# Seven products in every gate/up and down stage of a two-layer encoder trunk, and the rotary angles on GpSimd

## The chip, the cores and the metric

One core of one Trainium2 chip runs the whole program. The metric is the device time of one execution in microseconds (us), as the median of several runs of the same program. A time belongs to the program from its launch to its end; the profile of one execution has a span, from its first to its last instruction, which is a little shorter.

The engines are called as in the profile: PE is TensorE's matmul, PEld its weight load, DVE is VectorE, ACT is ScalarE, POOL is GpSimd, SP is SyncE, whose queue (SPq) issues every DMA of this kernel.

## The reference

Two layers on a sequence of 256 frames, model width 1024, all in float32. Each layer is a half-step feed-forward block, a mixer, and a second half-step feed-forward block:

```
def rmsnorm(x, g):  y = x * rsqrt(mean(x * x) + EPS);  return y * g
def swiglu(h, w_gate, w_up, w_down):                       # D_FF = 2816
    return (silu(h @ w_gate) * (h @ w_up)) @ w_down

for i in range(2):
    x = x + 0.5 * swiglu(rmsnorm(x, ffn1_norm[i]), ...)
    h = rmsnorm(x, mix_norm[i]);  q_s, k_s, v_s, q_m = split(h @ w_in[i])
    o_m = memory attention of q_m over mem (256 rows, 4 heads)
    o_s = chunked attention with relative bias    (i = 0)
        | differential attention with rotary      (i = 1)
    x = x + concat([o_s, o_m]) @ w_out[i]
    x = x + 0.5 * swiglu(rmsnorm(x, ffn2_norm[i]), ...)
```

The rotary tables need cos and sin of position times inverse frequency. Only layer 1's mixer uses them.

## The kernel before

**Precision by splitting.** A product of two float32 matrices is made of three passes of a faster format. Every operand is split into `hi` (rounded) and `lo` (the rest), and `dense()` (lines 489 to 506) issues three matmuls: `xh*wh` (L496), `xh*wl` (L499) and `xl*wh` (L502), each 128 x 128 against 128 x 512. Three such matmuls are called one dense step below. ACT makes `hi` (L326 for weights) and DVE makes `lo` (L344), so each weight that comes in costs work on both.

**Stages.** The four feed-forward blocks are (layer, block) = (0,1), (0,2), (1,1), (1,2). Each has a gate/up stage and a down stage. The gate/up stage has 11 groups of 256 columns. For each group there are two weight chunks (the two halves of the contraction), each holding 256 gate and 256 up columns; a chunk takes 8 dense steps (4 of k by 2 halves of the rows). `evac()` (from line 601) turns a finished group into `silu(gate) * up`, transposes it in blocks (L621), writes it to DRAM (`hd`, L627) and reads it back turned (`hr`, L632), and splits it into the operand `ht` (L641, L643). The down stage has 11 chunks of 8 dense steps, one for each group. Its last three chunks are run with the output quarter as the outer loop (lines 867 to 873), so that `finish()` (L577) can add one quarter to `x` and prepare the next stage's operand (`prep_half`, L531) while the others still run.

**Seven products for eight.** A block product of 2 x 2 blocks can be made of seven products instead of eight. The kernel has this in two places. In a gate/up stage, `PAIR` names a group; it and its successor form the 2 x 2 blocks, and `product()` (L799) runs seven products of 4 dense steps, so 28 instead of 32. For that, `pair_items()` (L385) needs sums of weight blocks (L338), `pair_forms()` (L746) sums of the activation's blocks, whose unrounded halves `y` are kept, and `pair_sums()` (L768) adds up the results. In a down stage, `SEVEN` names chunks: `seven_item()` (L377) makes four sums and seven splits of the chunk's four parts, `seven_forms()` (L648) the same of the activation, `seven()` (L675) runs 7 dense steps instead of 8, and `seven_sums()` (L686) adds four banks that all such chunks of a stage share into `x`, after the last of them. Before the change block (0,1) has neither.

**Buffers.** Raw weight chunks go through 3 buffers, split chunks through 4 (`whl`); a seven-product chunk takes two of the four, since it has seven parts. `Xt` is the transposed, split activation of a stage (two `xh` and two `xl` tiles); the next stage's is allocated ahead of the down stage (line 837). `g4` (12 slots) holds `ht` and its like, `g2` (19 slots) small tiles, and PSUM has 8 banks.

**Order of work.** Nothing is reordered at run time. The program is written out by `Flow` (L47), a small model of time with costs for each engine: PE work moves its clock by 0.216 for a matmul (`T_MM`), and generators ("threads") are resumed when their time has come. A generator that yields `flow.now + 3.0` places its next instruction that much later in the order. Idle threads (the weight loader, the two splitters, the rotary setup) are served after the others. `dense()` gives them a turn after each matmul. `calm` conditions let an instruction in only when the modelled DVE (or ACT) is free, or, with `SLACK`, nearly free. Each engine executes its instructions strictly in that written order; on a wrong guess of a transfer's time the engine waits, with all that is behind.

**Rotary setup.** `rope_setup()` (from L1057) waits until all small loads written so far have gone out, then runs one chain of small 128 x 64 steps on DVE (L1071 to L1116): position times frequency, the argument reduced by a constant in five pieces, each for a high and a low part. Every step waits until the modelled DVE is entirely free (`calm`, L1053). Two sines on ACT (L1119, L1120) and 16 steps on DVE (L1128, L1130) end it.

**Memory.** `memory_turn()` (L923) brings `mem` through DVE transposes to DRAM, `memory_prep()` (L949) reads it back and splits it, `memory_kv()` (L991) uses it right after block (0,1). POOL computes the `rsqrt` of all norms (L516) and the rotary products of layer 1 (L1219).

Of the kernel before, what the change touches and what calls it, by code (L numbers as in the profile page):

```python
# [12 lines left out]
F32 = mybir.dt.float32  # L13
F32R = mybir.dt.float32r
# [6 lines left out]
P = 128  # L21
# [121 lines left out]
def kernel(  # L143
# [101 lines left out]
    class Item:  # L245
# [3 lines left out]
        def __init__(self, raws, uses=8, w=1):  # L249
# [3 lines left out]
            self.n, self.frees, self.takes, self.gives = 1, 1, 0, 0  # L253
# [15 lines left out]
    hl_left = [NHL]  # L269
    dma_free = [2.3]  # L270
# [94 lines left out]
    SEVEN = {(0, 1): (), (0, 2): (1, 4, 6), (1, 1): (1, 4, 6), (1, 2): (1, 4, 7)}  # L365
    PAIR = {(0, 1): None, (0, 2): 3, (1, 1): 3, (1, 2): 3}
# [10 lines left out]
    def seven_item(it):  # L377
# [3 lines left out]
        it.n, it.uses, it.takes, it.gives = 2, 7, 4, 4  # L381
# [48 lines left out]
    def plan_ffn(l, nm, wg, wu, wd):  # L430
# [58 lines left out]
    def dense(ps, xh, xl, ready, c, need, start, stop):  # L489
# [14 lines left out]
        if c.uses == 0:  # L504
            hl_left[0] += c.n
        return flow.pe(T_MM)
# [88 lines left out]
    def ffn(l, nm, xt, gc_next):  # L595
# [5 lines left out]
        def evac(g, ps, end, gives=None):  # L601
# [27 lines left out]
            g2.give()  # L629
            yield g2.has()  # L630
# [206 lines left out]
        nxt = None if gc_next is None else Xt(nm == 2 and PAIR[l + 1, 1] is not None)  # L837
# [27 lines left out]
        if nm == 1:  # L865
            table_hint(AF.Exp)
        for tb in range(2):
# [81 lines left out]
    def memory_prep():  # L949
        yield g2.has(8)  # L950
# [102 lines left out]
    def calm(n, extra=0.0):  # L1053
        t = flow.dve(n, extra) + 0.3
        return lambda: flow.now >= t and flow.free["V"] <= flow.now

    def rope_setup():  # L1057
# [13 lines left out]
        nc.vector.tensor_copy(pf, pi)  # L1071
        yield calm(2)
        for tb in range(2):
            nc.vector.tensor_scalar(out=ang[:, tb * 32:(tb + 1) * 32], in0=invf, scalar1=pf[:, tb:tb + 1],
                                    scalar2=None, op0=ALU.mult)
            yield calm(n)
# [3 lines left out]
        nc.vector.tensor_copy(hi, hr.bitcast(F32))  # L1080
        yield calm(n)
        nc.vector.tensor_sub(lo, ang, hi)
        yield calm(n)
# [595 lines left out]
```

## Time and profile before

| | us |
|---|---|
| median of 3 runs | 961.64 |
| lowest, highest | 959.97, 965.21 |
| the profiled execution, its time | 962.03 |
| the profiled execution, its span | 960.3 |

| engine | busy, us | share of the span |
|---|---|---|
| PE | 948.0 | 99% |
| DVE | 806.0 | 84% |
| ACT | 577.8 | 60% |
| POOL | 63.1 | 7% |

The share is that of the whole span. A stage is read on its own: the windows of the trace give busy time for a stretch, the timeline gives single instructions with what ended the idle time before them (in brackets), and the list of waits says who waited for whom. Block (0,1) runs to about 192 us, layer 0's mixer to about 310, block (0,2) to about 495, block (1,1) to about 675, layer 1's mixer to about 775, and the rest is block (1,2).

### The profile page before, as it was taken

What the parts mean: (1) busy time and instruction counts of PE and PEld (TensorE: products, weight loads), DVE (VectorE), ACT (ScalarE), POOL (GpSimd) and SP (SyncE); (2) the same over time, 40 slices, a digit from 0 to 9 for tenths busy, and PEclk for the clock granted to TensorE, in tenths of its full rate; (3) what the DMA queues carried; (4) which work ended last, traced back from release to release, by engine and by line L of the source; (5) the groups of instructions that cost most, each with busy time, mean ns of one, the idle gap of its engine ahead of it and who ended that gap; (6) DMA issues with size and microseconds to landing.
All of it is one profiled execution on the core that took longest, in us unless ns stands there. A gap on an engine that the chain in (4) does not pass through costs nothing.

```text
span 960.3 us, 13252 instructions
## 1 busy us (share of the span) xinstructions
PE 948.0 (99%) x4489; PEld 776.9 (81%) x4489; DVE 806.0 (84%) x1532; ACT 577.8 (60%) x1100; POOL 63.1 (7%) x65
## 2 busy tenths in 40 slices
PE   8999999999999999999999999999999999999998
PEld 6888888888877888888888888887787788888886
DVE  6867777788877889979989988798989888997885
ACT  6655555566676656556646655554676866665651
POOL 1000000022110100000000000000334100000000
PEclk9999999999999999999999999999999999999999
DMA  8988868486435387786756678666541375688761
GB/s 275 332 256 273 278 229 274 154 272 210 158 107 174 92 262 226 233 289 221 234 184 201 219 231 263 221 234 224 187 165 45 126 223 183 211 258 261 240 230 44
DMA packets 169294, 204.02 MB, mean 212 GB/s; under 512 B 9674, under 2 KB 144395, under 8 KB 169227
## 3 DMA queue, kind: packets, MB, share of 16 engines
q1 hardware_dynamic: 169226, 203.18, 65.7%
q8 instruction: 35, 0.57, 0.2%
q14 instruction: 33, 0.26, 0.1%
HBM read 188.99 MB, written 14.16 MB: 212 GB/s over the span
## 4 chain that ended last, share of the span: by engine, by line
PE 87%; DVE 8%; DMA 2%; ACT 1%; SPq 1%; issue 1%; DVEq 0%; ACTq 0%
PE gu L502 14%; PE gu L499 14%; PE gu L496 14%; PE acc L496 8%; PE acc L502 8%; PE acc L499 8%; DVE lo L344 3%; PE pj L502 3%; PE pj L499 3%; PE pj L496 3%; PE pair_m L502 2%; PE pair_m L499 2%; PE pair_m L496 2%; PE xtp L509 1%; PE S L1320 1%; PE AV L1401 1%
## 5 line engine op out<-in xcount | busy, mean ns | idle before, releaser
L326 ACT CAST hi<-raw 128x512 fp32r<-128x512 f32 (+1 forms) x469 | 338.2, 771 | 160.9 <-DMA raw<-in_ffn_w_up_dram 43.4
L344 DVE TENSOR_TENSOR lo<-raw,hi 128x512 fp32r<-128x512 f32 (+1 forms) x469 | 393.0, 873 | 45.4 <-ACT hi L326 44.6
L502 PE MATMUL gu<-hi,xl 128*128 128x512 f32 x608 | 236.9, 390 | 0.0
L496 PE MATMUL gu<-hi,xh 128*128 128x512 f32 x608 | 236.8, 389 | 0.0
L499 PE MATMUL gu<-lo,xh 128*128 128x512 f32 x608 | 236.7, 389 | 0.0
L502 PEld LDWEIGHTS gu<-hi,xl 128*128 128x128 f32 x608 | 114.1, 188 | 23.7
L499 PEld LDWEIGHTS gu<-lo,xh 128*128 128x128 f32 x608 | 114.1, 188 | 23.6
L496 PEld LDWEIGHTS gu<-hi,xh 128*128 128x128 f32 x608 | 114.2, 188 | 23.5
L499 PE MATMUL acc<-lo,ht 128*128 128x512 f32 x280 | 110.1, 393 | 2.0 <-DVE lo L344 2.0
L496 PE MATMUL acc<-hi,ht 128*128 128x512 f32 x280 | 110.0, 393 | 0.0
L502 PE MATMUL acc<-hi,ht 128*128 128x512 f32 x280 | 109.9, 393 | 0.0
L502 PE MATMUL pj<-hi,xl 128*128 128x512 f32 x160 | 64.5, 403 | 0.0
L499 PEld LDWEIGHTS acc<-lo,ht 128*128 128x128 f32 x280 | 52.9, 189 | 13.7 <-DVE lo L344 2.9
L499 PE MATMUL pj<-lo,xh 128*128 128x512 f32 x160 | 63.6, 397 | 0.0
L496 PE MATMUL pj<-hi,xh 128*128 128x512 f32 x160 | 63.5, 397 | 0.0
L502 PEld LDWEIGHTS acc<-hi,ht 128*128 128x128 f32 x280 | 53.0, 189 | 11.0
L496 PEld LDWEIGHTS acc<-hi,ht 128*128 128x128 f32 x280 | 53.0, 189 | 10.9
L641 ACT CAST ht<-hr 128x512 fp32r<-128x512 f32 x35 | 21.7, 619 | 65.2 <-DMA hr<-hd 65.1
L326 ACT CAST hi<-wsum 128x512 fp32r<-128x512 f32 x84 | 49.2, 621 | 15.7 <-DVE wsum L338 12.3
L344 DVE TENSOR_TENSOR lo<-wsum,hi 128x512 fp32r<-128x512 f32 x84 | 53.0, 682 | 0.0
L610 ACT ACTIVATE sil<-gu,xr 128x256 f32<-128x256 f32 x76 | 35.7, 469 | 24.6 <-PE gu L502 24.1
L643 DVE TENSOR_TENSOR ht<-hr,ht 128x512 fp32r<-128x512 f32 x35 | 24.0, 687 | 26.1 <-ACT ht L641 26.0
(215 smaller groups left out, 1297.6 us busy)
## 6 DMA issues: line engine op xcount, KB each, us to landing
raw<-in_ffn_w_down_dram SPq DMA_DIRECT2D x176, 256.0 KB, 4.3
raw<-in_ffn_w_gate_dram SPq DMA_DIRECT2D x86, 512.0 KB, 4.6
raw<-in_ffn_w_up_dram SPq DMA_DIRECT2D x86, 512.0 KB, 5.7
raw<-in_w_in_dram SPq DMA_DIRECT2D x32, 512.0 KB, 5.9
hd<-hb SPq DMA_DIRECT2D x44, 256.0 KB, 4.9
hr<-hd SPq DMA_DIRECT2D x44, 256.0 KB, 3.7
raw<-in_w_out_dram SPq DMA_DIRECT2D x8, 1024.0 KB, 4.9
raw<-in_w_mem_kv_dram SPq DMA_DIRECT2D x4, 1024.0 KB, 5.6
```

The source lines that it names most:

```text
L326: nc.scalar.copy(out=it.part(0, q, w), in_=src())
L344: nc.vector.tensor_sub(it.part(1, q, w), src(), it.part(0, q, w).bitcast(F32))
L496: nc.tensor.matmul(out=ps, lhsT=xh, rhs=wh, start=start, stop=False)
L499: nc.tensor.matmul(out=ps, lhsT=xh, rhs=wl, start=False, stop=False)
L502: nc.tensor.matmul(out=ps, lhsT=xl, rhs=wh, start=False, stop=stop)
L509: nc.tensor.transpose(out=dst, in_=src, identity=flip if flipped else ident)
L610: nc.scalar.activation(sil, ps[tb][:, 0:256], AF.Silu, scale=xt.r[tb])
L641: nc.scalar.copy(out=hi, in_=src)
L643: nc.vector.tensor_sub(lo, src, hi.bitcast(F32))
L1320: nc.tensor.matmul(out=ss[e][:, pr, :nk], lhsT=q[rows, pr, :], rhs=k[rows, pr, :], start=i == 0, stop=i == len(passes) - 1)
L1401: nc.tensor.matmul(out=av[64 * e:64 * e + 64, pr, :], lhsT=vsrc(kb, pr, e), rhs=pts[e][:, pr, kb, :], start=(kb == 0), stop=(kb == nb - 1))
```

## The change

- `PAIR` of block (0,1) becomes 5, so that groups 5 and 6 run as seven products. `SEVEN` becomes (1, 5) there; in the other three it is (1, 4, 7), which it already was in (1,2), while (0,2) and (1,1) had (1, 4, 6).
- Of the seven-product chunks of a stage only the first still takes two split buffers. The others are "guests": four of their parts are in one split buffer, and the other three are in the tiles of `Xt`, which are free once the gate/up stage is done. One guest can be there at a time (`xt_room`), and the next stage's `Xt` is allocated after the down stage's eighth chunk.
- The last three down chunks are split in the order of parts 0, 2, 1, 3, unless they are seven-product chunks.
- The read-back `hr` of each group is placed 2.0 later in the order.
- All of the rotary chain ahead of the sines (95 steps) goes from DVE to POOL, with 0.25 as its cost in the model and no condition on DVE. The 16 steps behind the sines stay on DVE, with a looser condition.
- `memory_turn` has the looser condition too, and `memory_prep` waits until all four pieces of `mem` were written.

```diff
@@ class Item
-            self.n, self.frees, self.takes, self.gives = 1, 1, 0, 0
+            self.n, self.frees, self.takes, self.gives, self.guest = 1, 1, 0, 0, False
...
         def part(self, lo, q, w=1):
-            t = (self.lo if lo else self.hi)[q // 4]
-            return t[:, q % 4 * 512:(q % 4 + w) * 512]
+            ts = self.lo if lo else self.hi
+            if self.guest and q >= 4:
+                return ts[q // 2 - 1].rearrange("p k t -> p (k t)")[:, q % 2 * 512:(q % 2 + w) * 512]
+            return ts[q // 4][:, q % 4 * 512:(q % 4 + w) * 512]
@@ split_hi
-            yield lambda: hl_left[0] >= it.n and all(r.raw is not None for r in it.raws)
+            yield lambda: (hl_left[0] >= it.n and all(r.raw is not None for r in it.raws)
+                           and (xt_room[0] or not it.guest))
             hl_left[0] -= it.n
+            if it.guest:
+                xt_room[0] = False
...
+            if it.guest:
+                for x, ts in (("xh", it.hi), ("xl", it.lo)):
+                    ts += [xtp.tile([P, KT, P], F32R, tag=f"{x}{j}", name=f"g{x}{j}") for j in range(2)]
@@
-    SEVEN = {(0, 1): (), (0, 2): (1, 4, 6), (1, 1): (1, 4, 6), (1, 2): (1, 4, 7)}
-    PAIR = {(0, 1): None, (0, 2): 3, (1, 1): 3, (1, 2): 3}
+    SEVEN = {(0, 1): (1, 5), (0, 2): (1, 4, 7), (1, 1): (1, 4, 7), (1, 2): (1, 4, 7)}
+    PAIR = {(0, 1): 5, (0, 2): 3, (1, 1): 3, (1, 2): 3}
@@ plan_ffn
             if c in SEVEN[l, nm]:
-                seven_item(dn[-1])
+                seven_item(dn[-1], c != SEVEN[l, nm][0])
+            elif c >= NG - 3:
+                u = dn[-1].units
+                u[1], u[2] = u[2], u[1]
@@ evac
             g2.give()
+            yield flow.now + 2.0
             yield g2.has()
             hr = g2.take([P, 4, P], F32, "hr")
@@ ffn, ahead of the down stage
-        nxt = None if gc_next is None else Xt(nm == 2 and PAIR[l + 1, 1] is not None)
+        xt_room[0] = True
@@ ffn, after the eighth down chunk
+        assert xt_room[0]
+        xt_room[0] = False
+        nxt = None if gc_next is None else Xt(nm == 2 and PAIR[l + 1, 1] is not None)
@@ memory_turn, memory_prep
-                yield lambda: flow.free["V"] <= flow.now
+                yield lambda: flow.free["V"] <= flow.now + SLACK
...
-        yield g2.has(8)
+        yield lambda: len(memd) == 4 and g2.left >= 8
@@ rope_setup, each of its 95 steps ahead of the sines in this way
-                nc.vector.tensor_scalar(out=a, in0=part, scalar1=float(cval), scalar2=None, op0=ALU.mult)
-                yield calm(n)
+                nc.gpsimd.tensor_scalar(out=a, in0=part, scalar1=float(cval), scalar2=None, op0=ALU.mult)
+                yield flow.pool(0.25)
...
-                    yield calm(n)
+                    flow.dve(n, 0.06)
+                    t = flow.dve(n, 0.06) + 0.3
+                    yield lambda: flow.now >= t and flow.free["V"] <= flow.now + SLACK
```

More of the change, by code (lines that the diff above doesn't have):

```diff
@@ L269 @@
     hl_left = [NHL]
+    xt_room = [False]
     dma_free = [2.3]
@@ L375, with seven_item @@
     WO = (0, 1, 2, 3)
-    def seven_item(it):
+    def seven_item(it, guest):
         r = [it.own(q) for q in range(4)]
         t = lambda j: lambda: it.t[j]
-        it.n, it.uses, it.takes, it.gives = 2, 7, 4, 4
+        it.n, it.uses, it.takes, it.gives, it.guest = 1 if guest else 2, 7, 4, 4, guest
         it.sums = [(r[1], r[0]), (r[3], t(0)), (r[3], r[1]), (r[2], t(1))]
@@ L505, in dense @@
             hl_left[0] += c.n
+            xt_room[0] |= c.guest
         return flow.pe(T_MM)
@@ L1079, in rope_setup @@
         yield flow.act(n)
[L1080 to L1083 removed]
+        nc.gpsimd.tensor_copy(hi, hr.bitcast(F32))
+        yield flow.pool(0.25)
+        nc.gpsimd.tensor_sub(lo, ang, hi)
+        yield flow.pool(0.25)
         def frac(dst, src):
[L1086 to L1089 removed]
+            nc.gpsimd.tensor_scalar(out=b, in0=src, scalar1=MAGIC, scalar2=MAGIC, op0=ALU.add, op1=ALU.subtract)
+            yield flow.pool(0.25)
+            nc.gpsimd.tensor_sub(dst, src, b)
+            yield flow.pool(0.25)
         left = Fraction(TWO_PI_INV_NUM, TWO_PI_INV_DEN)
@@ L1110, in rope_setup @@
                     yield from frac(fa, a)
-                    nc.vector.tensor_add(acc, acc, fa)
-                    yield calm(n)
+                    nc.gpsimd.tensor_add(acc, acc, fa)
+                    yield flow.pool(0.25)
                     yield from frac(acc, acc)
         S2PI = 6.283185
-        nc.vector.tensor_scalar(out=a, in0=acc, scalar1=0.25, scalar2=None, op0=ALU.add)
-        yield calm(n)
+        nc.gpsimd.tensor_scalar(out=a, in0=acc, scalar1=0.25, scalar2=None, op0=ALU.add)
+        yield flow.pool(0.25)
         yield from frac(a, a)
```

28 lines of the change are left out of this document (10 added, 18 removed).

## The prediction, made before the changed kernel was run

> **What bounds the kernel now.** I read the page's busy times first, then PE's matmuls in the timeline, then PE's waits, then the windows by stage.
>
> ```profile
> span 960.3 us, 13252 instructions
> PE 948.0 (99%) x4489; PEld 776.9 (81%) x4489; DVE 806.0 (84%) x1532; ACT 577.8 (60%) x1100; POOL 63.1 (7%) x65
> ```
> ```profile
> 400.34 0.39 PE L496 MATMUL gu<-hi,xh 128*128 128x512 f32 x1
> ...
> 401.02 0.39 PE L496 MATMUL gu<-hi,xh 128*128 128x512 f32 x1
> ```
>
> A busy PE is not yet a PE at its peak, so the pitch matters. Between these two L496 lie an L499 and an L502, so three matmuls take 401.02 - 400.34 = 0.68 us, that is 0.227 us each and 0.68 us for one dense step. PE keeps this pitch nearly everywhere. In the list of its waits (total, times, longest) the first line here is the end of block (1,1)'s down stage, the other three lie in the mixers:
>
> ```profile
> PE acc L499 <- DVE lo L344: 2.0, 2, 1.2
> ...
> PE ptp L509 <- DVE pe L1447: 0.6, 1, 0.6
> PE acc L496 <- DVE oT L1308: 0.4, 1, 0.4
> PE qktp L509 <- DVE m L1226: 0.4, 1, 0.4
> ```
>
> That stage's end in the timeline, and DVE's load by stage (length, then PE, PEld, DVE, ACT and POOL busy, granted clock, transfers' share, GB/s):
>
> ```profile
> 656.58 0.39 PE L496 MATMUL acc<-hi,ht 128*128 128x512 f32 x1
> 658.13 0.50 PE L499 MATMUL acc<-lo,ht 128*128 128x512 f32 x1 [1.17 <-DVE lo L344]
> ...
> 659.94 0.69 PE L499 MATMUL acc<-lo,ht 128*128 128x512 f32 x1 [0.85 <-DVE lo L344]
> ...
> 662.99 0.63 PE L502 MATMUL acc<-hi,ht 128*128 128x512 f32 x1
> 663.42 0.43 PE L496 MATMUL acc<-hi,ht 128*128 128x512 f32 x1
> 663.69 0.39 PE L499 MATMUL acc<-lo,ht 128*128 128x512 f32 x1
> ```
> ```profile
> 24.00:120.00 96.00, 96.00 (x424) 79.24 (x423) 68.96 (x98) 53.02 (x82) 0.00 (x0) 1.00 0.91 285
> 120.00:192.00 72.00, 72.00 (x325) 59.60 (x325) 53.93 (x142) 40.13 (x80) 2.59 (x4) 1.00 0.67 219
> 336.00:432.00 96.00, 96.00 (x425) 79.54 (x424) 86.71 (x141) 53.84 (x82) 0.00 (x0) 1.00 0.79 252
> 432.00:504.00 72.00, 72.00 (x327) 59.61 (x326) 66.71 (x127) 43.14 (x80) 1.38 (x2) 1.00 0.67 213
> 648.00:672.00 24.00, 21.99 (x93) 17.42 (x92) 19.37 (x32) 11.50 (x22) 0.00 (x0) 0.93 0.70 227
> ```
>
> PE waits twice for a weight's `lo` from DVE, 2.0 us in all, and then its matmuls start 0.43 apart (662.99 to 663.42) up to there, while the granted clock of that window is 0.93 instead of 1.00. Thirteen matmuls lie between 656.58 and 663.69: 7.11 us, where 13 x 0.227 = 2.95 would do. The stall costs 4.2 us: half of it is waiting, half the slow matmuls behind. The Trainium skill (TensorE: Matmul & The Clock Gate, Part 1) puts the fall to half clock down to an idle window of about 3.4 us; by that, these two waits cost their own 2.0 us alone, and the sum below would be 955.9. The trace disagrees: waits of 1.17 and 0.85 us went before the halved pitch. So PE bounds the kernel, DVE comes next, and one DVE stall is in the way.
>
> **Products.** Block (0,1) is the one without seven products. Its pair takes 7 x 4 = 28 dense steps for 32, and its two down chunks 7 for 8 each: 6 dense steps, 18 matmuls, 6 x 0.68 = **4.1 us** of PE. In the other three blocks the count is the same (three chunks before and after). PE is the bound, so this comes off the end if nothing else is late.
>
> What feeds it costs DVE. For the pair, block (0,2)'s gate/up window, which has one, is the comparison: 86.7 us of DVE in 96, against 69.0 in block (0,1). The price is so 17.7 us, and DVE stays at 87 of 96 (memory's transposes are in the 69.0 already). In (0,2) PE ran 96.00 of 96.00 with it. The pair's four operand forms are due only at group 5, and the halves `y` exist from the stage's start. For the down stage:
>
> ```profile
> L344 DVE TENSOR_TENSOR lo<-raw,hi 128x512 fp32r<-128x512 f32 x303 | 194.8, 686 | 23.7 <-ACT hi L326 23.6
> L338 DVE TENSOR_TENSOR wsum<-raw,wsum 128x512 f32<-128x512 f32 x42 | 27.9, 682 | 0.2
> L690 DVE SCALAR_TENSOR_TENSOR x<-msum,x 128x512 f32<-128x512 f32 x12 | 8.3, 688 | 0.2
> L657 DVE TENSOR_TENSOR sf<-hr 128x128 f32<-128x128 f32 x18 | 5.0, 278 | 0.0
> L1088 DVE TENSOR_TENSOR ropew<-ropew 128x64 f32<-128x64 f32 x20 | 4.4, 221 | 0.2
> ```
>
> Each seven-product chunk adds 4 sums and 3 splits (7 x 0.68 = 4.8), 4 forms (1.1) and two more, narrower `ht` splits (0.28 to 0.69 each, some 0.7 together): 6.6 us; the final sums are 8 steps of 0.69, 5.5. For two chunks 2 x 6.6 + 5.5 = 18.7 us. The rotary chain gives back, in 120 to 192, by the timeline, 38 of its 95 steps at 0.2 = 7.6. So 53.9 + 18.7 - 7.6 = 65 us of DVE in 72: tight, not over.
>
> **The rotary chain on POOL.** Over the whole span DVE loses 95 x 0.2 = 19 us of work. No POOL step of 64 columns stands in the trace; the nearest:
>
> ```profile
> L1219 POOL TENSOR_TENSOR m<-qkn,ropeS 128x256 f32<-128x256 f32 x12 | 11.2, 954 | 7.2 <-ACT hi L326 3.0 <-DVE rs L1439 2.0 <-ACT k L1252 1.2
> L200 POOL TENSOR_SCALAR_AFFINE_SELECT flip<-flip 128x128 f32<-128x128 f32 x1 | 0.3, 292 | 0.1
> ```
> ```profile
> 121.67 0.16 DVE L1071 CAST pos_f<-pos_i 128x2 f32<-128x2 int32 x1
> 173.07 1.28 ACT L878 ACT_TABLE_LOAD   x1
> 189.91 0.55 POOL L516 TENSOR_TENSOR xr<-v,nhalf 128x1 f32<-128x1 f32 x1 [66.34 <-DVE v L514]
> ```
>
> Bounds for one step: 0.29 (one input, twice the columns) and 0.95 (two inputs, four times the columns). I take 0.4, an estimate nearer the first, as the columns are half of its and more than half of the chain has one input. How the chain is written out sets its pace: each step is resumed 0.25 + 0.22 = 0.47 later in the model, and the model looks every 0.216, so after three matmuls, 3 x 0.227 = 0.68 us on the chip. From about 121 us that makes 95 x 0.68 = 65 us, to about 186. At 0.4 POOL keeps up, is done before `xr` is due at 190, and the sines find their input. They then fall behind the load of the other function table at 173, so two more loads of 1.28 may come, 0 to 2.6 us of ACT; ACT is busy 40 of 72 there, and 32 dense steps of `memory_kv` (22 us) that need no new `x` cover it. If that cover were gone, it would be 2.6 us of PE.
>
> POOL can also slow DVE:
>
> ```profile
> L1222 DVE TENSOR_TENSOR m<-qkn,ropeC 128x512 f32<-128x512 f32 x6 | 5.9, 988 | 0.0
> L1226 DVE TENSOR_TENSOR m<-m,m 128x512 f32<-128x512 f32 x6 | 4.1, 684 | 0.0
> ```
>
> Both are two-input steps of one size; L1222 runs beside POOL's products and takes 0.30 more. Six of these, 1.8 us, against 11.2 us of POOL: 0.16 of POOL's time. With 95 x 0.4 = 38 us of POOL, DVE loses 6 us, 71 of 72 in that window; the lower end is nothing. The upper end, that POOL stops DVE for all of its time, is a rival below.
>
> **The stall of 656 us.** It has a history:
>
> ```profile
> 608.79 0.36 SPq L632 DMA_DIRECT2D hr<-hd  x1
> ...
> 612.80 0.62 ACT L641 CAST ht<-hr 128x512 fp32r<-128x512 f32 x1 [6.62 <-DMA hr<-hd]
> 613.45 0.69 DVE L643 TENSOR_TENSOR ht<-hr,ht 128x512 fp32r<-128x512 f32 x1 [3.93 <-ACT ht L641]
> ...
> 640.03 0.18 DVE L1130 SCALAR_TENSOR_TENSOR ropeS<-gqk,ropew 128x32 f32<-128x32 f32 x1
> ```
>
> The read-back landed late, ACT idled 6.6 us and DVE 3.9 behind it, with weights queued behind both. Placing `hr` and all that follows it 2.0 later gives back about 2 us of that. On SP, raw weights that stood behind the waiting read-back go out earlier; the `ht` of a group is needed many chunks later, so its own delay costs nothing. The 14 last rotary steps between 608 and 640, about 0.1 us apart, are long done: 1.4 us. The order 0, 2, 1, 3 takes one 0.69 us split out of the first quarter's way. Together 4.1 us of DVE against 2.0 of waiting: I take the stall as gone, **4.2 us**. Against that, the sums (5.5 us) move from chunk 6 to chunk 7, one chunk (8 x 0.68 = 5.4 us) nearer the end.
>
> **Costed at nothing.** The second guest's splits must wait until the first guest's chunk is used; two plain chunks lie between (16 x 0.68 = 10.9 us) for 7 splits and 4 sums (7.5 us of DVE). Without them up to 7.5 us would show. The later `Xt`, the looser conditions and the wait for the fourth memory piece move no due work.
>
> **Sum.** 962.0 (the profiled execution, 0.4 above the median of the runs, which scatter by 5) - 4.1 - 4.2 = **953.7**. I leave the 0.4 out.
>
> **Rivals.**
>
> *Stall stays or moves (0.24).* DVE has 67 us of 72 in block (0,2)'s down stage already, and the sums come later; an equal stall at 660 or at another boundary gives 962.0 - 4.1 = 957.9. Against it: block (1,2) runs with (1, 4, 7) and shows no such wait.
>
> *DVE overruns in 120 to 192 (0.09).* If POOL holds it up for 10 us, DVE needs 75 of 72: 3 us of waiting, doubled by the slow matmuls as at 656. 953.7 + 6 = 959.7.
>
> *POOL shuts DVE out (0.03).* If the two-input steps of both never run together, DVE loses up to 38 us: 103 in 72, 31 late. Two split chunks ahead (16 x 0.68 = 11 us) cover part of it; PE loses 20 and 2 of slow matmuls, 976. Against it: L1222 lost 1.8 us, not 11.2. The Trainium skill (SBUF — State Buffer, Who interferes with whom) has this as a rule and so speaks against the change: a DVE step with two SBUF inputs and a POOL step that reads SBUF exclude one another. By that, 976; the trace agrees in direction only.
>
> *Products do not shorten block (0,1) (0.05).* The transfers' share is 0.91 in 24 to 120. If weights set the pace there, the 4.1 us stay: 957.8. Against it: PE is full in that window.
>
> *POOL lags (0.10), slower.* ACT executes in order, and the sines are behind POOL's chain. At 0.95 a step the chain ends at 121 + 90 = 211, ACT stands from 186 to 211, 25 us, with every weight split behind it. The same 11 us of cover leave 14 for PE, and 2 of slow matmuls: 970. It costs more than the gain of 8.3 once ACT stands for 17.3 us, so from (65 + 17.3) / 95 = 0.87 us a step. For it: L1219. Against it: L200.
>
> **Chances.** The forecast has the remaining 0.49. Its own range is 951.9 (the 1.4 us of short waits in the mixers and the 0.4 of the profiled execution gone too) to 956 (half of the stall left). 0.5% of 961.6 is 4.8 us, about what a measurement of this kernel can tell from no change; below 956.8 is faster, above 966.4 slower. Faster: the forecast and 0.02 of the stall's rival, 0.51. Slower: POOL's two, 0.13. The same: the rest, 0.36. The range leaves out POOL's two and a little at either end: 951.9 to 962 (959.7 and a second short stall).
>
> **What would show it.** PE: 4489 - 18 = 4471 matmuls, 32 dense steps fewer on `gu` and 28 more on `pair_m`, at the pitch of 0.227. No wait of PE for `lo` near 652, and granted clock 1.00 there. DVE near 87 in 24 to 120 and below 72 in 120 to 192. POOL steps of 0.3 to 0.5 us, ended before 190, and ACT's sines without a long wait for POOL. Wrong: a long ACT wait for POOL near 186, new PE waits for `lo` in block (0,1), or two-input DVE steps well above 0.69 between 121 and 186.

## The result, and the profile after

| | before | after |
|---|---|---|
| median, us (4 runs each, on one chip) | 960.81 | 974.69 |
| lowest, highest | 959.16, 965.21 | 971.05, 975.17 |
| the profiled execution, its time | 962.03 | 975.17 |
| the profiled execution, its span | 960.3 | 973.4 |

The changed kernel is slower: the ratio is 1.014 with a 95% interval of 1.0118 to 1.0161. The forecast of 953.7, its range up to 962 and the sign were wrong.

In the code after the change the three matmuls of a dense step stand at L508, L511 and L514, the weights' `lo` at L353 and `hi` at L335, the weights' sums at L347, memory's transposes (`mb`) at L936 and the preparation's `meml` at L987. The page's first lines of after:

```profile
span 973.4 us, 13318 instructions
PE 950.7 (98%) x4471; PEld 776.1 (80%) x4471; DVE 837.6 (86%) x1516; ACT 592.4 (61%) x1132; POOL 118.4 (12%) x160
```

There are 18 matmuls fewer, as forecast, and yet PE's busy time rose from 948.0 to 950.7, so some matmuls ran slowly; and the span has 22.7 us without PE, where it had 12.3. DVE shows 31.6 us more work. The list of PE's waits of after (for whom; total, times, longest):

```profile
PE kv L514 <- DVE meml L987: 5.1, 2, 3.8
PE m L511 <- DVE lo L353: 2.6, 1, 2.6
PE xtp L522 <- DVE x L596: 2.2, 1, 2.2
PE gu L511 <- DVE lo L353: 2.1, 1, 2.1
PE acc L511 <- DVE lo L353: 1.8, 2, 1.5
```

All five are waits for DVE: `gu` in a gate/up stage, `m` in a seven-product chunk, `acc` in a down stage, `xtp` at the start of what follows, `kv` in memory's products. Where they lie, the windows of after answer (the same five as in the prediction; length, then busy time of PE, PEld, DVE, ACT and POOL, granted clock, transfers' share, GB/s):

```profile
24.00:120.00 96.00, 93.88 (x406) 76.84 (x405) 82.65 (x129) 54.46 (x89) 0.00 (x0) 0.98 0.78 248
120.00:192.00 72.00, 65.33 (x287) 52.65 (x286) 66.64 (x116) 43.56 (x84) 48.78 (x85) 1.00 0.79 262
336.00:432.00 96.00, 96.00 (x427) 79.50 (x426) 89.60 (x141) 60.55 (x91) 0.94 (x1) 1.00 0.75 235
432.00:504.00 72.00, 72.00 (x321) 59.61 (x320) 61.02 (x103) 37.80 (x71) 0.00 (x0) 1.00 0.72 235
648.00:672.00 24.00, 24.00 (x107) 19.88 (x106) 19.83 (x37) 14.87 (x27) 0.00 (x0) 1.00 0.76 248
```

The last line is the good news: where PE had 21.99 of 24 at a clock of 0.93, it has 24.00 at 1.00. The stall near 656 us is gone. The first two lines are the bad news: PE was full in block (0,1), and now it lacks 2.1 us in the gate/up stage and 6.7 in the down stage. DVE looks harmless in both, 82.65 of 96 and 66.64 of 72, less than its 89.60 in block (0,2), where PE misses nothing. That is the reading that deceives here, and the experiments are about it.

One measure serves for all that follows. If each matmul of a dense step starts 0.227 us behind the last, as nearly all do, then what a gap has beyond that is lost time of PE, whether it was a wait or a slow matmul. Added up over the whole trace, this is 19.5 us before and 37.0 after, 17.5 more. Less the 18 matmuls saved (4.1), that leaves 13.4, and the spans differ by 13.1: the account closes. By place (us lost):

| | gate/up (0,1) and the first seven-product chunk, 48 to 144 | rest of the down stage, 144 to 192 | memory's products, 192 to 240 | 648 to 672 |
|---|---|---|---|---|
| before | 0.2 | 0.4 | 0.9 | 4.4 |
| after | 7.8 | 4.4 | 8.8 | 0.0 |

### The profile page after: what moved, and what is told of

The parts are those of the page before. It is cut to its first block, busy times and chain, and to the rows that moved or that the text cites. A ratio compares the mean times of both kernels' runs of the same rounds, so it can differ in the third digit from the quotient of the medians.

```text
span 973.4 us, 13318 instructions
## 1 busy us (share of the span) xinstructions
PE 950.7 (98%) x4471; PEld 776.1 (80%) x4471; DVE 837.6 (86%) x1516; ACT 592.4 (61%) x1132; POOL 118.4 (12%) x160
## 4 chain that ended last, share of the span: by engine, by line
PE 72%; DVE 15%; DMA 6%; ACT 2%; issue 2%; SPq 2%; ACTq 0%; DVEq 0%
PE gu L514 10%; PE gu L511 10%; PE gu L508 10%; DVE lo L353 7%; PE acc L508 7%; PE acc L511 7%; PE acc L514 7%; PE pj L514 2%; PE pj L511 2%; PE pj L508 2%; DMA raw<-in_ffn_w_up_dram 2%; PE pair_m L511 2%; PE pair_m L514 2%; PE pair_m L508 2%; ACT hi L335 2%
## 5 line engine op out<-in xcount | busy, mean ns | idle before, releaser
L335 ACT CAST hi<-raw 128x512 fp32r<-128x512 f32 (+1 forms) x465 | 335.0, 770 | 175.9 <-DMA raw<-in_ffn_w_up_dram 42.0
L353 DVE TENSOR_TENSOR lo<-raw,hi 128x512 fp32r<-128x512 f32 (+1 forms) x465 | 391.3, 878 | 33.1 <-ACT hi L335 33.1
L511 PE MATMUL gu<-lo,xh 128*128 128x512 f32 x576 | 225.2, 391 | 2.2 <-DVE lo L353 2.1
L514 PE MATMUL gu<-hi,xl 128*128 128x512 f32 x576 | 225.2, 391 | 0.4 <-DVE xl L559 0.4
L508 PE MATMUL gu<-hi,xh 128*128 128x512 f32 x576 | 225.0, 391 | 0.0
L511 PEld LDWEIGHTS gu<-lo,xh 128*128 128x128 f32 x576 | 108.6, 188 | 25.9 <-DVE lo L353 3.3
L514 PEld LDWEIGHTS gu<-hi,xl 128*128 128x128 f32 x576 | 108.4, 188 | 22.9 <-DVE xl L559 0.8
L508 PEld LDWEIGHTS gu<-hi,xh 128*128 128x128 f32 x576 | 108.6, 189 | 22.6
L511 PE MATMUL acc<-lo,ht 128*128 128x512 f32 x264 | 103.1, 391 | 1.8 <-DVE lo L353 1.8
L514 PE MATMUL acc<-hi,ht 128*128 128x512 f32 x264 | 103.4, 392 | 0.0
L508 PE MATMUL acc<-hi,ht 128*128 128x512 f32 x264 | 103.0, 390 | 0.0
L335 ACT CAST hi<-wsum 128x512 fp32r<-128x512 f32 x87 | 51.2, 619 | 37.9 <-DVE wsum L347 35.2
L511 PE MATMUL pj<-lo,xh 128*128 128x512 f32 x160 | 64.0, 400 | 0.0
L508 PE MATMUL pj<-hi,xh 128*128 128x512 f32 x160 | 63.9, 399 | 0.0
L514 PE MATMUL pj<-hi,xl 128*128 128x512 f32 x160 | 63.8, 399 | 0.0
L529 POOL TENSOR_TENSOR xr<-v,nhalf 128x1 f32<-128x1 f32 x12 | 10.8, 901 | 429.9 <-DVE v L527 429.9
L511 PEld LDWEIGHTS acc<-lo,ht 128*128 128x128 f32 x264 | 49.6, 188 | 13.0 <-DVE lo L353 2.6
L508 PEld LDWEIGHTS acc<-hi,ht 128*128 128x128 f32 x264 | 49.6, 188 | 10.1
L514 PEld LDWEIGHTS acc<-hi,ht 128*128 128x128 f32 x264 | 49.6, 188 | 10.0
L353 DVE TENSOR_TENSOR lo<-wsum,hi 128x512 fp32r<-128x512 f32 x87 | 56.2, 682 | 0.0
L529 POOL TENSOR_TENSOR hf<-v,nhalf 128x8 f32<-128x8 f32 (+1 forms) x20 | 31.5, 1577 | 96.4 <-DVE v L527 88.2
```

Source lines behind the costliest of these rows:

```text
L335: nc.scalar.copy(out=it.part(0, q, w), in_=src())
L353: nc.vector.tensor_sub(it.part(1, q, w), src(), it.part(0, q, w).bitcast(F32))
L508: nc.tensor.matmul(out=ps, lhsT=xh, rhs=wh, start=start, stop=False)
L511: nc.tensor.matmul(out=ps, lhsT=xh, rhs=wl, start=False, stop=False)
L514: nc.tensor.matmul(out=ps, lhsT=xl, rhs=wh, start=False, stop=stop)
L529: nc.gpsimd.tensor_tensor(out=dst, in0=v[:, :n], in1=nhalf[:, :n], op=ALU.pow)
```

## The experiments

Four explanations stood against each other. **Volume**: DVE has more to do in block (0,1) than it has time. **Order**: DVE has room, but memory's preparation is let in too late by its strict condition. **Supply**: the three raw buffers, freed late, let the load's own time show. **POOL**: the chain on POOL holds up DVE or ACT. Each run below was compared with the kernel before on the same chip; its medians lay between 959.64 and 961.26.

### One part at a time

**The rotary chain back on DVE** (`e1_rope_dve`), with the looser condition:

```diff
-                nc.gpsimd.tensor_sub(a, a, fa)
-                yield flow.pool(0.25)
+                nc.vector.tensor_sub(a, a, fa)
+                yield calm(n)          # calm: flow.free["V"] <= flow.now + SLACK
```

> The changed kernel with the 95 rotary steps back on DVE, let in when the modelled DVE is nearly free (the looser condition of the change). Theory POOL (the rotary steps on POOL hold up DVE's two-input steps, and that is what makes DVE late in block (0,1)): `lo` splits between 141 and 208 us fall from 0.745 to 0.685 us, the PE waits at 181, 186 and in the memory products shrink, 965 to 969 us. Theory VOLUME (the products of block (0,1) bring DVE more work than it has room for there, whoever does the angles): DVE gets 95 x 0.2 us back in the same stretch, the waits stay or grow, 973 to 979 us.

Measured: 972.09 (970.38 to 973.91), ratio 1.0122 [1.0098, 1.0145]. That lies between the two ranges expected. The waits stay (`kv` 5.4 us, `gu` 2.8, `m` 2.7), so POOL is not what makes PE wait. The median is 2.6 us below that of after, although DVE has 5.7 us more to do (843.3 busy for 837.6); but the runs and the intervals of the two overlap, so it is not shown that the chain on POOL costs time. What the rows do show is that it makes DVE's steps longer. The steps of L353 between 141 and 208 us, first of after, with the chain beside them on POOL, then of this kernel (count, busy, mean ns):

```profile
L353 DVE TENSOR_TENSOR lo<-raw,hi 128x512 fp32r<-128x512 f32 x52 | 36.1, 745 | 1.0 <-ACT hi L335 1.0
```
```profile
L353 DVE TENSOR_TENSOR lo<-raw,hi 128x512 fp32r<-128x512 f32 x53 | 33.7, 684 | 0.8 <-ACT hi L335 0.8
```

Beside POOL a step takes 745 ns, without it 684: 52 x 0.061 = 3.2 us in these steps. Summed in the same way over all groups of DVE steps that both windows hold, it is some 5 us, an estimate.

**No pair in block (0,1)** (`e2_no_pair`), **no seven-product chunks there** (`e3_no_seven`), **neither** (`e5_neither`):

```diff
-    SEVEN = {(0, 1): (1, 5), ...
-    PAIR = {(0, 1): 5, ...
+    SEVEN = {(0, 1): (), ...        # e3, e5
+    PAIR = {(0, 1): None, ...       # e2, e5
```

> The changed kernel without the gate/up pair in block (0,1); its down chunks 1 and 5 stay seven products. Theory VOLUME: the wait at 102 us with its slow matmuls (4.0 us) goes, the 4 dense steps come back (2.7 us), the down stage starts less late: 969 to 974 us. Theory POOL: nothing but the products changes, 976 to 978 us.

> The changed kernel without seven-product down chunks in block (0,1); the pair stays. Theory VOLUME: 18.7 us of DVE work leave the stretch from 136 to 200 us, so the waits at 138, 181, 186 and those of the memory products (17 us with the slow matmuls) go and 2 dense steps (1.4 us) come back: 958 to 962 us. Theory POOL: only the wait at 138 (3.5 us) goes: 972 to 974 us.

> The changed kernel with neither the pair nor the seven-product down chunks in block (0,1): left are the angles on POOL, the guests with (1, 4, 7), the later read-back and the order of the last three chunks' parts. If these parts have no cost of their own in block (0,1), only the stall at the end of block (1,1) goes from the kernel before (4.2 us): 955.5 to 957.5 us. If the angles on POOL or the guests cost by themselves: 959 us or more.

| | median, us | range | ratio [95%] | DVE busy | lost, 48 to 144 | 144 to 192 | 192 to 240 |
|---|---|---|---|---|---|---|---|
| after (both) | 974.69 | 971.05 to 975.17 | 1.014 [1.0118, 1.0161] | 837.6 | 7.8 | 4.4 | 8.8 |
| e2, sevens only | 957.18 | 957.07 to 959.68 | 0.9972 [0.9958, 0.9986] | 812.4 | 0.2 | 0.4 | 2.8 |
| e3, pair only | 962.42 | 960.9 to 964.85 | 1.0018 [1.0002, 1.0034] | 821.0 | 4.0 | 0.5 | 1.3 |
| e5, neither | 957.15 | 956.54 to 958.01 | 0.9957 [0.9937, 0.9976] | 795.7 | 0.2 | 0.4 | 1.0 |

`e3_no_seven` and `e5_neither` came out within 0.5 us of what volume and no cost of the rest would give. The expectation for `e2_no_pair` missed by 12 us: it said 969 to 974 if volume is the cause, and so left the sevens a loss of their own. They have none, and the two parts do not add up. Against neither, the sevens alone change nothing, the pair alone costs 5.3 us, and both together cost 17.5. More than three times the sum says that something fills up. The column of DVE says how much: the pair is 821.0 - 795.7 = 25.3 us of DVE, by the other path 837.6 - 812.4 = 25.2; the two sevens are 812.4 - 795.7 = 16.7. (The profiled execution of `e2_no_pair`, 959.68, was its slowest; its losses are those of that one.) Where the work falls, the windows from 120 to 192 of `e5_neither`, `e2_no_pair` and `e3_no_seven` show:

```profile
120.00:192.00 72.00, 72.00 (x325) 59.62 (x324) 50.40 (x105) 41.78 (x83) 46.63 (x99) 1.00 0.69 220
120.00:192.00 72.00, 72.00 (x325) 59.62 (x324) 63.61 (x120) 43.06 (x86) 52.66 (x99) 1.00 0.70 229
120.00:192.00 72.00, 69.41 (x307) 55.95 (x306) 58.37 (x114) 43.33 (x86) 43.36 (x85) 1.00 0.77 261
```

The sevens bring DVE 63.61 - 50.40 = 13.2 us there, and the pair, whose last product ends at 124.5 us, still 58.37 - 50.40 = 8.0.

### Volume or order

**Memory's preparation let in sooner** (`e4_mem_slack`), and the same without the pair (`e17_no_pair_slack`):

```diff
-                yield lambda: flow.free["A"] <= flow.now
+                yield lambda: flow.free["A"] <= flow.now + SLACK
...
-                yield lambda: flow.free["V"] <= flow.now
+                yield lambda: flow.free["V"] <= flow.now + SLACK
```

> The changed kernel with the looser condition (nearly free in place of free) on the two steps of memory's preparation. Theory ORDER (the memory operand's splits are let in only when the modelled DVE and ACT are free, which a full DVE never is, so they come last and the memory products wait): the two waits of the memory products and their slow matmuls (9 us) go, 964 to 967 us. Theory VOLUME alone: the same DVE work is only in another order, the weights' `lo` come later instead, 972 to 977 us.

> The changed kernel without the pair in block (0,1) and with the looser condition on memory's preparation. Without the pair one wait of the memory products is left (1.8 us) because their splits wait for a free DVE: if DVE has room for them, it goes and 955 to 956.5 us are left; if not, it moves to the weights' `lo` and the time is 957 us or more.

Measured: `e4_mem_slack` 979.08 (978.17 to 979.93), ratio 1.0194 [1.0176, 1.0212], which is worse than after and above both ranges expected. The first two lines of PE's waits in `e4_mem_slack`:

```profile
PE acc L511 <- DVE lo L353: 9.2, 7, 2.1
PE m L511 <- DVE lo L353: 2.3, 1, 2.3
```

The waits of `kv` are gone, and seven waits of `acc` have come: the lost time is now 7.5, 10.4 and 5.9 in the three places. Let in sooner, the preparation pushes aside the splits of the down stage. Without the pair the same edit gives 957.96 (956.63 to 961.0), ratio 0.997 [0.9953, 0.9987], where 955 to 956.5 was expected if DVE had room. The one wait of `kv` is gone, but 3.1 us are lost in 192 to 240 for the 2.8 of `e2_no_pair`, now around other waits for DVE (`qktp` 1.2 us, `xtp` 0.6). So nothing was gained even there: order is not the cause; it only chooses who is late.

**Memory's DVE work taken away** (`e12_no_mem_dve`): an ACT copy stands in for each transpose, and a second ACT copy for `meml`, so that the memory attention is computed from other values. With less on the modelled DVE, the written order shifts a little too.

```diff
-                yield lambda: flow.free["V"] <= flow.now + SLACK
-                t = turn_blocks(xb[:, :, tb], m[:, tb])
+                t = flow.act(256, 0.1)
+                nc.scalar.copy(out=xb[:, :, tb].rearrange(...), in_=m[:, tb].rearrange(...))
...
-                yield lambda: flow.free["V"] <= flow.now
-                for tb in range(2):
-                    nc.vector.scalar_tensor_tensor(out=lo[:, tb], ...)
-                    tt[kk] = flow.dve(128, 0.06)
+                nc.scalar.activation(lo, src, AF.Copy, scale=g)
+                tt[kk] = flow.act(256)
```

> The changed kernel with the memory input's DVE work left out: its block transposes become plain copies on ACT, and the `lo` part of its operand is written by ACT as a second copy (so the memory attention is computed from other values). 8 x 0.61 + 32 steps of together 9 to 11 us, some 15 us, leave DVE between 60 and 215 us; every transfer stays. Theory VOLUME (DVE has too much work in block (0,1) with pair, seven products and memory together): most of the 17 us of waits go, 957 to 963 us. Rival SUPPLY (weights arrive late in block (0,1), since the pair keeps raw buffers and small loads and memory's transfers stand between the weights on SP): 970 to 974 us.

Then each half alone, only the transposes off DVE (`e21_no_turn`) and only the preparation off DVE (`e22_no_prep`):

> The changed kernel with only memory's block transposes taken off DVE (plain copies on ACT, 8 x 0.61 = 4.9 us of DVE between 64 and 120 us; the memory attention is computed from other values). Theory LOCAL PEAK (DVE is full where the pair and the transposes fall together, and starts the down stage late): the waits at 102 and 138 us (7.5 us with slow matmuls) go, and the later ones shrink by what is no longer carried over: 958 to 967 us. Theory LATE PREPARATION (the late `lo` of the memory operand makes most of the loss): 969 to 973 us, with the waits of the memory products left.

> The changed kernel with only the `lo` part of the memory operand taken off DVE (a second copy on ACT; 32 steps, 9 to 11 us of DVE between 160 and 222 us; the memory attention is computed from other values). LOCAL PEAK: the waits at 102 and 138 stay (7.5 us), those from 181 on go or shrink: 964 to 969 us. LATE PREPARATION: 957 to 963 us.

| | median, us | range | ratio [95%] | lost, 48 to 144 | 144 to 192 | 192 to 240 |
|---|---|---|---|---|---|---|
| e12, neither on DVE | 957.89 | 956.46 to 960.96 | 0.997 [0.9948, 0.9992] | 0.2 | 2.7 | 1.0 |
| e21, no transposes on DVE | 965.93 | 965.53 to 966.58 | 1.0068 [1.0051, 1.0085] | 0.2 | 3.4 | 8.1 |
| e22, no preparation on DVE | 967.64 | 965.57 to 971.28 | 1.0089 [1.0065, 1.0112] | 6.6 | 2.4 | 1.1 |

With pair and sevens in place, 12.8 us of DVE less (824.8 for 837.6) give back 16.8 us of time. Each half takes away the loss at its own place: the transposes that of the gate/up stage, the preparation that of memory's products. (Without the transposes the loss in memory's products hardly shrinks, 8.1 for 8.8, so it is not only carried over from the gate/up stage.) By the medians the halves give back 8.8 and 7.0 us, 15.8 of the 16.8; measured against the kernel before on each chip, which was 1.2 us lower on that of the halves, 7.6 and 5.9 of 17.0. This is the shown cause: DVE's volume. The windows of `e12_no_mem_dve` also give the demand that after's windows hide, because in them nobody is late:

```profile
24.00:60.00 36.00, 36.00 (x160) 29.68 (x159) 28.87 (x42) 20.63 (x28) 0.00 (x0) 1.00 0.90 285
60.00:120.00 60.00, 60.00 (x265) 49.41 (x264) 56.48 (x91) 40.25 (x76) 0.00 (x0) 1.00 0.78 249
```

The second of these stretches in after, with its counterpart in block (0,2), and then its first half in pieces of 12 us, also of after:

```profile
60.00:120.00 60.00, 57.88 (x248) 47.15 (x247) 53.88 (x88) 33.72 (x61) 0.00 (x0) 0.97 0.71 226
372.00:432.00 60.00, 60.00 (x266) 49.67 (x266) 57.12 (x93) 38.44 (x57) 0.00 (x0) 1.00 0.80 252
```
```profile
60.00:72.00 12.00, 12.00 (x55) 9.94 (x54) 11.93 (x20) 6.93 (x14) 0.00 (x0) 1.00 0.61 187
72.00:84.00 12.00, 12.00 (x55) 9.86 (x53) 8.92 (x13) 6.32 (x13) 0.00 (x0) 1.00 0.89 296
84.00:96.00 12.00, 12.00 (x54) 9.72 (x53) 11.97 (x23) 8.65 (x12) 0.00 (x0) 1.00 0.55 174
```

DVE's load without the transposes is 56.5 us of the 60. The eight transposes of `mem` (L936) all lie in that stretch, from 66.9 to 118.2 us in after, and take 4.6: 61.1 of 60, an estimate from these two rows. Block (0,2) asks 57.1 of 60 there and loses nothing. What DVE has free ahead of the stretch, 36.00 - 28.87 = 7.1 us, does not help: the transfers' share is 0.90 there, and in after ACT waits 7.2 us for raw weights between 24 and 60, so hardly more work is to be had there.

A DVE that is full does not show as 100% for long, because it chokes its own supply: 11.93 of 12, then 8.92 of 12. The chain of after between 60 and 106 us tells why (start, length, what):

```profile
70.44 1.13 DVE lo L353
...
71.94 0.04 SPq L291
...
72.02 7.47 DMA raw<-in_ffn_w_up_dram
...
80.68 2.36 DVE lo L353 x2
```

DVE frees a raw buffer with its last split; only then SP issues the next load, which takes 7.47 us; meanwhile DVE runs dry, and what it missed comes on top later. The same stands ahead of PE's first wait. SP issues the next loads at 93.66 and 94.09, right behind DVE's split that ends at 93.64; ACT waits 5.03 us for them, until 98.99; DVE then waits twice for ACT, and comes to the split that PE needs only at 103.75:

```profile
91.29 5.76 DVE L353 TENSOR_TENSOR lo<-raw,hi 128x1024 fp32r<-128x1024 f32 x5
...
94.09 0.50 SPq L291 DMA_DIRECT2D raw<-in_ffn_w_up_dram  x1
...
98.99 1.05 ACT L335 CAST hi<-raw 128x1024 fp32r<-128x1024 f32 x1 [5.03 <-DMA raw<-in_ffn_w_up_dram]
...
101.78 0.48 DVE L626 SCALAR_TENSOR_TENSOR h<-gu,xr,sil 128x256 f32<-128x256 f32 x1 [1.03 <-ACT sil L623]
...
102.48 0.39 PE L508 MATMUL gu<-hi,xh 128*128 128x512 f32 x1
102.78 0.69 DVE L657 TENSOR_TENSOR ht<-hr,ht 128x512 fp32r<-128x512 f32 x1 [0.51 <-ACT ht L655]
...
103.75 2.32 DVE L353 TENSOR_TENSOR lo<-raw,hi 128x1024 fp32r<-128x1024 f32 x2
...
104.99 0.50 PE L511 MATMUL gu<-lo,xh 128*128 128x512 f32 x1 [2.12 <-DVE lo L353]
...
107.36 0.63 PE L514 MATMUL gu<-hi,xl 128*128 128x512 f32 x1
107.78 0.63 PE L508 MATMUL gu<-hi,xh 128*128 128x512 f32 x1
```

### Supply, and places to put the work

**A fourth raw buffer** (`e13_raw4`; `g2` gives up four slots for it):

```diff
-    NRAW, NHL, NT2 = 3, 4, 19
+    NRAW, NHL, NT2 = 4, 4, 15
```

> The changed kernel with four raw weight buffers in place of three; the room comes from the small tiles (15 in place of 19). SUPPLY: weights can be fetched one chunk further ahead, the waits at 102 and 138 us go and much of what follows, 958 to 966 us. VOLUME: DVE's work is the same, 970 to 978 us.

Measured: 969.48 (967.84 to 971.32), ratio 1.0078 [1.0051, 1.0106], between the two ranges expected. The wait of `gu` near 102 is gone, as the chain above would have it, but `m` waits 3.3 us and `kv` 4.9: lost 6.9, 1.2 and 8.8, for 7.8, 4.4 and 8.8. The buffer is worth some 5 us: supply is part of the way in which a full DVE makes PE wait, but 12 of the 17.5 us stay with the fourth buffer.

**Memory's transposes later** (`e19_mem_later`) and **the pair earlier** (`e11_pair3`), to keep the two apart:

```diff
-        yield lambda: at[0] >= 8
+        yield lambda: at[0] >= 18          # e19, memory_turn
-    PAIR = {(0, 1): 5, ...
+    PAIR = {(0, 1): 3, ...                 # e11
```

> The changed kernel with memory's transposes begun ten weight chunks later (after chunk 18 in place of 8), so behind the pair. LOCAL PEAK: the wait at 102 us (4 us) goes, since DVE has only the pair there; the same 4.9 us of work then stand in the way of the down stage, whose waits and those of the memory products grow: 965 to 985 us in all. If the wait at 102 us stays, the transposes were not its cause.

> The changed kernel with the pair of block (0,1) at groups 3 and 4, where the other blocks have it. Theory VOLUME with a local peak (the pair's DVE work and memory's transposes fall into the same 40 us, 64 to 105): the pair's steps come some 20 us earlier, in front of most of memory's, so the waits at 102 and 138 us shrink and less is carried into the down stage: 962 to 970 us. If the load of the whole block decides and not its peak: 973 to 977 us.

Measured: `e19_mem_later` 971.45 (969.72 to 974.54), ratio 1.0128 [1.0108, 1.0148]; `e11_pair3` 969.66 (967.47 to 972.77), ratio 1.0098 [1.0064, 1.0133]. The first nearly empties the gate/up stage of losses (1.3) and fills memory's products (12.1); the second loses 8.3, 4.9 and 1.6. The medians are 3 and 5 us below that of after, the first of them not clear of the scatter. Neither cures: neither of the two places has room for all of it.

**The preparation on POOL** (`e14_mem_pool`), in 64 steps, each placed behind the one before, with the rotary chain behind them:

```diff
-                yield lambda: flow.free["V"] <= flow.now
...
-                    nc.vector.scalar_tensor_tensor(out=lo[:, tb], ...)
+                    nc.gpsimd.tensor_scalar(out=mtmp[:, tb], in0=src[:, tb], scalar1=g, ...)
+                    flow.pool(0.6)
+                    nc.gpsimd.tensor_sub(lo[:, tb], mtmp[:, tb], hi.bitcast(F32)[:, tb])
+                    tt[kk] = flow.pool(0.6)
+                yield tt[kk]
```

> The changed kernel with the `lo` part of the memory operand made on POOL (a product and a difference, 64 steps) with no condition on DVE, and the rotary chain begun only after it. VOLUME: 9 to 11 us leave DVE between 150 and 222 us, the waits of the memory products (9 us with their slow matmuls) go and those at 181 and 186 shrink, 960 to 967 us; those at 102 and 138 (7.5 us) stay. If POOL's reading beside DVE costs as much as the steps did: 972 us or more.

Measured: 988.93 (987.33 to 989.35), ratio 1.0274 [1.0235, 1.0314], the worst of all. Its waits of PE:

```profile
PE kv L514 <- POOL meml L989: 7.4, 7, 2.8
PE kv L508 <- ACT memh L984: 5.5, 3, 2.5
```

The edit made the preparation a serial chain: each ACT step of `memh` is placed behind the POOL steps of the one before, and the chain ended even later. 24.3 us are lost in memory's products. The run missed and says nothing on volume.

### What took the stall at 656 us away

Two parts of the change alone, in the kernel before: the read-back 2.0 later (`e6_before_hr`), and the chain on POOL (`e7_before_pool`).

```diff
             g2.give()
+            yield flow.now + 2.0                    # e6, in evac
             yield g2.has()
...
-                nc.vector.tensor_sub(a, a, fa)
+                nc.gpsimd.tensor_sub(a, a, fa)      # e7, all of rope_setup as in after
```

> The kernel before with one edit, the read-back `hr` placed 2.0 later in the order. Theory LATE READ-BACK (the stall at the end of block (1,1) comes from DVE idling behind a read-back that has not landed): the two waits and their slow matmuls go, 956 to 957.5 us. If the stall comes from DVE's load there (rotary steps, sums, split buffers): 960 to 961.5 us, with the stall still there.

> The kernel before with one edit, the rotary chain on POOL. If POOL's steps cost nothing where DVE has room, and the 14 rotary steps between 608 and 640 us are what makes DVE late at the end of block (1,1): 956 to 957.5 us. If they only lighten DVE where it has room anyway: 960 to 961.5 us. If POOL holds DVE up so that PE waits in block (0,1): 963 us or more.

Measured: `e6_before_hr` 957.16 (957.0 to 959.15), ratio 0.9974 [0.9961, 0.9987]; `e7_before_pool` 957.46 (957.11 to 958.37), ratio 0.9965 [0.9952, 0.9977]. The window of the old stall, in the one and in the other:

```profile
648.00:672.00 24.00, 24.00 (x113) 19.84 (x112) 19.31 (x33) 12.97 (x25) 0.55 (x1) 1.00 0.53 175
```
```profile
648.00:672.00 24.00, 24.00 (x113) 19.87 (x112) 19.32 (x34) 12.87 (x26) 0.55 (x1) 1.00 0.53 175
```

Either is enough. That is why the two best kernels, `e5_neither` and `e6_before_hr`, have one and the same time: both are in effect the kernel before without that stall, some 0.3 to 0.4% faster, and nothing that was tried in block (0,1) adds to it.

## Why the prediction was wrong

**Products: right in PE's work.** 4471 matmuls at a pitch of 0.227, 4.1 us less work. `e12_no_mem_dve` has them all, and its span is 955.7 against 955.8 of `e5_neither`: its other losses, 18.7 us against 14.6 over the trace, eat exactly the 4.1. The largest is the end of block (0,1), 2.7 us in 144 to 192 for 0.4. So no run here shows these products as time gained.

**The stall at 656: right.** 4.4 us lost became 0.0, and each of two causes that the prediction added together suffices alone (`e6_before_hr`, `e7_before_pool`).

**DVE in the gate/up stage: the step that failed.** It read: "The price is so 17.7 us, and DVE stays at 87 of 96 (memory's transposes are in the 69.0 already)." The pair costs DVE 25.3 us. The price had been taken as one window less another, 86.7 in (0,2) less 69.0 in (0,1), and then added to 69.0 again: that gives back (0,2)'s own 86.7, whatever lies in (0,1). The transposes that (0,1) has and (0,2) has not, 4.6 us, were so cancelled, not counted; what the other 3 us are was not worked out. Counting steps, as was done for the down stage, would have found it. The list of DVE's groups has, for `e3_no_seven` and then `e5_neither`:

```profile
L353 DVE TENSOR_TENSOR lo<-wsum,hi 128x512 fp32r<-128x512 f32 x82 | 52.7, 678 | 0.0
L347 DVE TENSOR_TENSOR wsum<-raw,wsum 128x512 f32<-128x512 f32 x50 | 33.1, 678 | 0.2
L347 DVE TENSOR_TENSOR wsum<-raw,raw 128x512 f32<-128x512 f32 x32 | 19.8, 677 | 2.0 <-DMA raw<-in_ffn_w_up_dram 2.0
```
```profile
L353 DVE TENSOR_TENSOR lo<-wsum,hi 128x512 fp32r<-128x512 f32 x66 | 42.5, 679 | 0.0
L347 DVE TENSOR_TENSOR wsum<-raw,wsum 128x512 f32<-128x512 f32 x42 | 27.8, 678 | 0.2
L347 DVE TENSOR_TENSOR wsum<-raw,raw 128x512 f32<-128x512 f32 x24 | 14.7, 675 | 0.0
```

16 splits and 16 sums more are 10.2 + 5.3 + 5.1 = 20.6 us; the sums of the results and of the activation are most of the rest. With all of the 25.3 on top of the 69.0 the stage would stand at 94.3 of 96, and its first third can't be filled: in `e3_no_seven` DVE has 83.9 us done in 24 to 120, and 8.0 us of the pair's work fall behind it, into the down stage.

**DVE in the down stage: the sevens right, the sum wrong.** "53.9 + 18.7 - 7.6 = 65 us of DVE in 72: tight, not over." The sevens cost 16.7 where 18.7 was said, 13.2 of it in this window. The rotary chain gave back 2.3 there and not 7.6 (53.93 before, 51.60 in `e7_before_pool`). And the 65 take for granted that the stage begins with nothing left over, where 8.0 us of the pair come on top. By the three windows above, 50.4 + 13.2 + 8.0 = 71.6 of 72: full, an estimate, with memory's preparation in it. So the rival "DVE overruns in 120 to 192" came nearest in mechanism, with the wrong origin (the pair, not POOL), and its 959.7 was 15 us too low: it priced one place, and three were late.

**"Costed at nothing": wrong for memory's preparation.** It is the last to be let in, only when the modelled DVE is free. Before, `meml` was made between 156.65 and 183.4 us, now between 184.6 and 223.3, while its products begin at 200.1. The new wait for the fourth piece is not why: `e5_neither` has it too, and makes `meml` between 156.5 and 183.2. The looser condition was not given to it, and `e4_mem_slack` shows that it would not have helped. The end of the wait, as PE's timeline of after has it:

```profile
213.08 0.39 PE L511 MATMUL kv<-lo,memh 128*128 128x512 f32 x1
217.30 0.50 PE L514 MATMUL kv<-hi,meml 128*128 128x512 f32 x1 [3.83 <-DVE meml L987]
...
219.55 0.80 PE L514 MATMUL kv<-hi,meml 128*128 128x512 f32 x1 [1.29 <-DVE meml L987]
...
222.33 0.63 PE L514 MATMUL kv<-hi,meml 128*128 128x512 f32 x1
222.75 0.63 PE L508 MATMUL kv<-hi,memh 128*128 128x512 f32 x1
```

**POOL: the step within its bounds, the end not.** The groups of the chain on POOL in after (count, busy, mean ns), one of the slowest and one of the faster:

```profile
L1099 POOL TENSOR_SCALAR ropew<-ropew 128x64 f32<-128x64 f32 x20 | 14.0, 701 | 1.7
L1101 POOL TENSOR_TENSOR ropew<-ropew 128x64 f32<-128x64 f32 x20 | 8.9, 445 | 1.7
```

0.4 was taken, and the means of the groups are 0.42 to 0.70. The one-input steps, thought cheaper, are mostly the dearer ones. The chain also stood 11.3 us for ACT's first rounding and ended at 207.6, not 186. The late end was harmless: it lay ahead of nothing that was due (`xr` came at 198.6, between two of its steps), and the two extra table loads came, at 207.66 and 246.26. The slowing of DVE was put at 6 us and is 3.2 in the steps of L353, some 5 in all. The Trainium skill (SBUF — State Buffer, Who interferes with whom) has DVE's steps with two SBUF inputs and POOL's that read SBUF exclude one another. The rows of L353 above agree in direction only: 3.2 us lost beside 52.59 us of busy POOL between 141 and 208.

**What stays open.** The pair alone (`e3_no_seven`) has a median 5.3 us above neither. Its profiled execution shows 3.7 of that (spans of 959.5 and 955.8), nearly all of it accounted for: 4.2 more lost between 48 and 240, 2.0 more elsewhere, 2.7 saved; the other 1.6 lies between profiled execution and median. Whether the chain on POOL cost this kernel time is not settled (`e1_rope_dve`). In `e13_raw4` the gain of the raw buffer and the loss of four `g2` slots were not separated. A version that makes the same transposes on another engine was not tried.

## What to carry to other kernels

Price an added piece by counting its steps; the difference of two windows cancels whatever only one of them holds. Before adding to the second-busiest engine, read its load in pieces as long as the buffers last, and ask which idle time can be filled at all: at 57 of 60 us nothing was lost here, and where some 61 of 60 were asked, PE lost 7.8 us in that stage and just behind it. When two edits that are harmless alone, or nearly so, cost three times their sum together, look for the engine that they share, and test by taking a third party's work off it.

## What the runs showed of the hardware

**A wait may cost twice its length, or not.** In after the wait of 2.12 us at 102.48 to 104.99 was followed by matmuls 0.43 apart (107.36 to 107.78), and the granted clock of 96 to 120 was 0.93; 4.0 us were lost in that window for 2.3 of the wait itself. The longer wait of 2.65 us at 138.38 was not followed by any:

```profile
141.42 0.50 PE L511 MATMUL m<-lo,h 128*128 128x512 f32 x1 [2.65 <-DVE lo L353]
...
142.22 0.39 PE L511 MATMUL acc<-lo,h 128*128 128x512 f32 x1
142.45 0.40 PE L514 MATMUL acc<-hi,h 128*128 128x512 f32 x1
```

These start 0.23 apart. The Trainium skill (TensorE: Matmul & The Clock Gate, Part 1) speaks of a free-running window of about 3.4 us; a window that runs free of the program would let equal waits end differently, as these do, but both waits are shorter than the window, and the first did slow PE down.

**POOL's small steps.** 128 x 64 elements took POOL 0.42 to 0.70 us (means of the groups), and the chain's steps followed each other by 0.64; a step of 128 x 32 took 0.62 (L1087), so half the columns were not cheaper.

**Moving a chain off DVE frees less than its steps.** 95 steps of about 0.2 us left DVE in `e7_before_pool`, and its busy time fell by 806.0 - 797.2 = 8.8 us, not 19. The traces say why: in that of before, 8.2 of the 19.0 us that these steps last lie under DVE's other steps, so that without them 795.2 would be left; and beside POOL the weights' splits became longer, by 2.1 us together. So the mean time of a small step, times count, does not give its price.
